# A two-layer hybrid attention trunk: projections of the next head pair move ahead of the gate, and scores that are not ready are passed over

## The chip, the core and the metric

The kernel runs on one core of one Trainium2 chip. The metric is the device time of one execution in microseconds (us); lower is better. The core has five instruction queues that run side by side and meet at semaphores: PE (TensorE, the matrix engine), DVE (VectorE), ACT (ScalarE), POOL (GpSimd) and SP (SyncE, which issues all DMAs here). Each queue runs its own instructions in the order in which they stand in the program.

## The reference, cut to what matters

Two layers of the following, on 1040 rows (16 learned meta tokens and 1024 inputs) of width 1024:

```python
hn = rmsnorm(h, norm_gain[l])
dq, dk, dv, dg, fq, fk, fv, ff, fg = jnp.split(hn @ w_in[l], split_points, axis=-1)
# four "diff" heads: two softmaxes per head, subtracted; q and k are rotated first
a = p[:, :, 0] - lam * p[:, :, 1]
do = rmsnorm(a @ dv, subln_gain[l]) * (1.0 - lam_init) * silu(dg)
# eight "fox" heads: causal softmax with a running sum of log-forget values as bias
log_f = jax.nn.log_sigmoid(ff + forget_bias[l])
cum_logf = jnp.cumsum(log_f, axis=1)
s = fq @ fk.T * scale + cum_logf[q] - cum_logf[k]
fo = (softmax(s) @ fv) * silu(fg)
h = h + concat([do, fo]) @ w_out[l]
```

## The kernel before

The rows are cut into 9 blocks and the blocks into 3 chunks of 336, 384 and 320 columns. The heads are worked in 8 pairs: pairs 0 to 3 are the diff heads, pairs 4 to 7 the fox heads. A layer runs on PE as two streams that are woven together:

- **Attention** (`attention`, `Unit`): for pair p and chunk c, scores (`scores`, PSUM tile `sc`), softmax on DVE and ACT (`e`, `mn`), transposes of the weights (`tp`, evicted by ACT and DVE as `ath` and `atl`), and the product with v (`po`). While the transposes and products of one unit run, the scores of the next unit `nx` are emitted between them.
- **Projections** (`fills`): units k, q, g (gate) and v, in the order of the string `ORDER`, which is cut by `|` into one segment for each pair. k0, for example, is the k projection of pair 0: three chunks of 24 matmuls each into a PSUM tile `pj`. There are two `pj` buffers. v2 also projects the 8 forget columns `ff`.

A matmul of two float32 matrices is made of three products of high and low parts, so every weight tile is loaded by DMA (`wst`), copied to `whi` (ACT or POOL) and subtracted to `wlo` (POOL or DVE). There are 4 buffers of `wst` and 8 each of `whi` and `wlo`; a v unit uses all 8, the others 4.

The order of PE's instructions is written out while the program is built: a planner in `layer` keeps an estimated clock `pe.t` and, each time that attention yields, emits projection steps in proportion to what is left of each stream. Attention names a key that must exist (`("k", p, c)`, say); if it does not, projection units are emitted until it does. A projection unit may yield `True`, which means that it has to wait for something: `k_unit` until the pair before the last has begun its scores, `q_unit` for chunk c until the scores of the pair before have used the buffer `ql` of that chunk. In that case `fills` takes the next gate out of the list and runs it as `other` in the place of the waiting unit, a step of 6 matmuls at a time; when the waiting unit can go on, `other` stays where it is until a unit waits again. The other engines' instructions are ordered by a scheduler of the build.

After the last step of v2, `log_forget` emits a chain of small DVE operations (and one exponential on ACT) on the forget columns, tile `ffz`, and returns the function `cumulate`. That one loads a triangular table with a DMA into a tile `tc` (3 buffers, of which the chain itself uses all three) and makes the running sum with matmuls `sc<-tc,ffz`, which need both the table and the chain's last result. `fills` calls it at a place of its own choice: before, when the unit behind v2 (k4) is finished. The unit `h` in the list works in the same way for the norms of the diff heads.

Of the kernel before, what the change touches and what calls it, by code (L numbers as in the profile page):

```python
# [42 lines left out]
LOP = [1, 1, 1, 1, 1, 1, 0, 0, 0, 1, 1, 0]  # L43


ORDER = ("k0 q0 k1 q1 | g0 k2 v1 q2 | g1 k3 q3 | g2 v2 k4 q4 | g3 k5 q5 | g4 v3 h k6 q6 | k7 q7 g5 | "
         "g6 g7")

START = "T0 S0 N0 x2 S1 T1 N1 v v v v v v S2 T2 N2 v v v v v v"

# [3 lines left out]

LS, LSC, LT, L1S, LROT, LFOX = ((1.9, 0.0033), (3.4, 0.0042)), 0.7, 2.4, 4.87, 8.0, 5.61
OT1, OT2, OT3, OW, OL = 2.46, 4.57, 2.54, 7.53, 4.52
CMAX, SLACK, RMIN, RMAX, STEP, FR0, FR1 = 3.17, 0.4, 0.03, 2.52, 2, 2, 2
COST = {"k": 11.4, "q": 11.4, "g": 11.4, "v": 25.7, "h": 0.0}
FADD = [0.0, 0.0, 0.0, 0.0, 0.0, 0.0, 0.0, 20.0]
# [25 lines left out]
def trunk_kernel(ctx, tc, x, meta, norm_gain, w_in, fbias, lq1, lk1, lq2, lk2,  # L85
# [87 lines left out]
    pe = Clock()  # L173
    const = {}
    when = {}
# [308 lines left out]
    def v_unit(l, u, acts, box):  # L484
        diff = u < 2
        v0 = (DV if diff else FV) + (u % 2) * 256
        cols = [(v0, v0 + 256)]
        n = 256
        ff = u == 2
        if ff:  # L490
            cols.append((FF, FF + 8))
            n = 264
        while u and box.get("vp", 0) < 2 * u - 1:
            yield True
        ws = load_w_all(w_in[l], cols)
        vt = [sb.tile([P, NB, 256], F32R, name="v", tag="v", bufs=3) for _ in range(2)]
        if ff:
            z = st("ffz", NB * 8, bufs=1)
            nc.vector.memset(z, 0.0)
        for j in range(NB):  # L500
            c = j // 3
            while acts[c] is None:
                yield True
            hi, lo = acts[c]
            sz = BE[j] - BS[j]
            pad = 64 if j == NB - 1 else 0
            o = BS[j] - CS[c] - pad
            m = sz + pad
            pt = proj_ps()
            i = 0  # L510
            for k in range(KT):
                wh, wl = ws[k]
                for a, b in ((hi, wh), (hi, wl), (lo, wh)):
                    mm(pt[:m, :n], a[:, k, o:o + m], b[:, :n], i == 0, i == 3 * KT - 1)
                    i += 1
                if k == 3:
                    yield
            for s in range(2):
                src = pt[pad:m, s * P:(s + 1) * P]
                if pad:  # L520
                    nc.gpsimd.memset(vt[s][0:pad, j, :].bitcast(F32), 0.0)
                if diff:
                    vh, vl = vt[s][pad:m, j, 0:P], vt[s][pad:m, j, P:2 * P]
                else:
                    src = src.rearrange("p (h d) -> p h d", h=2)
                    vv = vt[s][pad:m, j, :].rearrange("p (h x d) -> p h x d", h=2, x=2)
                    vh, vl = vv[:, :, 0, :], vv[:, :, 1, :]
                split(vh, vl, src, 1.0 if diff else 0.5)
            if ff:
                nc.vector.tensor_tensor(z[:sz, j * 8:(j + 1) * 8], pt[pad:m, 256:264],  # L530
                                        fb[:sz, l, :], ALU.add)
            box["v", 2 * u, j], box["v", 2 * u + 1, j] = vt
            when["v", 2 * u, j] = when["v", 2 * u + 1, j] = pe.t + 2.0
            if ff and j == NB - 1:
                box["lf"] = log_forget(l, z)
            yield

    def log_forget(l, z):

        n = NB * 8  # L540
        az = st("tc", CW)[:, :n]
        nc.vector.scalar_tensor_tensor(az, z, -1.0, z, ALU.mult, ALU.max)
        e = st("tc", CW)[:, :n]
        nc.scalar.activation(e, az, AF.Exp, scale=-1.0)

        d = st("tc", CW)[:, :n]
        nc.vector.tensor_scalar(d, e, 2.0, None, ALU.add)
        nc.vector.reciprocal(d, d)
        s = az
        nc.vector.tensor_tensor(s, e, d, ALU.mult)  # L550
        w = d
        nc.vector.tensor_tensor(w, s, s, ALU.mult)
        q = e
        nc.vector.tensor_scalar(q, w, 1.0 / 15, None, ALU.mult)
        for i in (13, 11, 9, 7, 5, 3):
            nc.vector.scalar_tensor_tensor(q, q, 1.0 / i, w, ALU.add, ALU.mult)
        nc.vector.scalar_tensor_tensor(q, q, 1.0, s, ALU.add, ALU.mult)
        nc.vector.tensor_scalar(z, z, 0.0, None, ALU.min)
        nc.vector.scalar_tensor_tensor(z, q, -2.0, z, ALU.mult, ALU.add)

        def cumulate():
            crow = big("cb", 2)
            upper = st("tc", CW)
            dma(out=upper[:, 0:P], in_=cst[:, C_U:C_U + P])
            for c in range(3):
                pt = proj_ps("sc")
                for j in range(3 * c, 3 * c + 3):
                    sz = BE[j] - BS[j]
                    o = BS[j] - CS[c]
                    mm(pt[:8, o:o + sz], z[:sz, j * 8:(j + 1) * 8], upper[:sz, :sz], True, True, 4)  # L570
                for j in range(3 * c, 3 * c + 3):
                    o = BS[j] - CS[c]
                    sz = BE[j] - BS[j]
                    prev = crow[:8, BS[j] - 1:BS[j]] if j else zero1[:8, :]
                    nc.vector.tensor_scalar(crow[:8, BS[j]:BE[j]], pt[:8, o:o + sz], prev, None,
                                            ALU.add)
            dma(out=cscr[l], in_=crow[:8, :])
        return cumulate


# [224 lines left out]
    def attention(l, box):  # L805
# [5 lines left out]
        def score(u, step):  # L811
# [7 lines left out]
                        dma(out=cb, in_=cscr[l, h:h + 1, :].to_broadcast([P, T]))  # L819
            u.score(*step)  # L820

        late = []
        todo = units[0].score_steps()
        yield 0.0, ("k", 0, 0)
# [4 lines left out]
        for i, u in enumerate(units):  # L829
            nx = units[i + 1] if i + 1 < len(units) else None  # L830
            todo = nx.score_steps() if nx else []
            free = EB - 3
            if nx and nx.diff:
                free = 2 * free - 1
            if nx and nx.p != u.p and not nx.diff:
                free = 0
            n = u.nblk
            seq = [("t", j) for j in range(TB)]
            for j in range(n):
                seq.append(("a", j))  # L840
                if j + TB < n:
                    seq.append(("t", j + TB))
            nt = 0
            yield u.ready, ("v", u.p, 0)
            box["vp"] = u.p
            for k, (what, j) in enumerate(seq):
                if late and pe.t >= late[0][0]:
                    late.pop(0)[1]()
                    yield 0.0, None
                if what == "t":  # L850
                    u.transp(j)
                    nt += 1
                else:
                    yield u.ev[j][2], ("v", u.p, j)
                    u.av(j)
                yield 0.0, None
                if todo and (nt == n or (free > 0 and nt >= FR0 and k % FR1 == FR1 - 1)):
                    free -= 1
                    yield 0.0, ("k", nx.p, nx.c)
                    yield pe.evicted[0], ("q", nx.p, nx.c)  # L860
                    score(nx, todo.pop(0))
                    yield 0.0, None
            for t0, f in late:
                yield t0, None
                f()
            late = u.finish()
            while todo:
                yield 0.0, ("k", nx.p, nx.c)
                yield pe.evicted[0], ("q", nx.p, nx.c)
                score(nx, todo.pop(0))  # L870
                yield 0.0, None
# [151 lines left out]
    def fills(l, acts, box, new):  # L1023

        unit = {"k": k_unit, "q": q_unit, "g": gate, "v": v_unit}
        todo = ORDER.replace("|", "").split()
        other = None
        while todo:
            u = todo.pop(0)
            now = head_norms(l, box) if u == "h" else unit[u[0]](l, int(u[1]), acts, box)  # L1030
            for r in now:
                if r and other is None:
                    g = next((x for x in todo if x[0] == "g"), None)
                    if g and u[0] != "v":
                        todo.remove(g)
                        other = gate(l, int(g[1]), acts, box)
                if r and other is not None:
                    r = next(other, "end")
                    if r == "end":
                        other, r = None, True  # L1040
                yield r
            if "lf" in box and u[0] not in "vh":
                box.pop("lf")()
            if other is not None and (not todo or todo[0][0] == "v"):
                yield from other
                other = None
# [67 lines left out]
    with tc.manual_schedule(engines={mybir.EngineType.PE}):  # L1114
        acts = [None] * 3
        box = {"done": {}, "sc_ok": set(), "fin": set(), "kept": 0, "sums": 0}
# [83 lines left out]
```

## Time and profile before

| | |
|---|---|
| time, median of 3 runs | 1607.41 us (1606.68 to 1609.51) |
| profiled execution: time, span | 1607.66 us, 1605.6 us |
| PE busy | 1487.7 us, 93% of the span |
| DVE, ACT, POOL busy | 1043.0, 828.6, 689.6 us |
| granted TensorE clock, mean of the span | 0.973 |

The span runs from the first to the last instruction; 2.1 us of the profiled time lie around it. The clock is granted as a share of 2.4 GHz. It takes one of two levels, 2.4 or 1.2 GHz, so a mean of 0.91 over a stretch says that 18% of it passed at 1.2 GHz, and at a steady stream of matmuls such a stretch does 9% less work.

### The profile page before, as it was taken

Reading aid. Unit: us, or ns where it says so; the run is one execution under the profiler, and the core shown is the slowest. Engines: PE = TensorE matmul, PEld = TensorE weight load, DVE = VectorE, ACT = ScalarE, POOL = GpSimd, SP = SyncE. Lnnn points to the kernel's source line nnn. Section 1 sums busy time; section 2 is a strip of 40 time slices with the busy share of each in tenths; the row PEclk is TensorE's granted clock in tenths of the full one; section 3 lists DMA queues with packets and bytes.
Section 4 is the critical chain, followed back from the end, with each engine's and each line's share of the span. In section 5 each row is a group of like instructions: output and inputs, shape, how many; then the busy total and the mean of one; then the engine's idle time right before and its main releaser. Section 6 shows DMA issues by size and latency. Waiting matters only on the chain. (4 is left out here: it accounts for less than half of the span.)

```text
span 1605.6 us, 30162 instructions
## 1 busy us (share of the span) xinstructions
PE 1487.7 (93%) x9932; PEld 1420.1 (88%) x9932; DVE 1043.0 (65%) x3024; ACT 828.6 (52%) x2067; POOL 689.6 (43%) x1125
## 2 busy tenths in 40 slices
PE   5988999999999999988998999899999999888997
PEld 4888989999999999887988899799999999886897
DVE  6488747866755575757655976586756555547564
ACT  6455545545654565543334654465556556446443
POOL 3353233404442445456846341442253344344674
PEclk9999999999999999998999999999999999999999
DMA  9252212223321324555434231332242222335454
GB/s 242 64 113 73 71 51 75 72 36 86 69 66 42 79 67 126 170 151 159 147 70 106 69 87 33 88 81 50 43 93 59 52 69 61 87 96 159 138 158 139
DMA packets 181725, 148.28 MB, mean 92 GB/s; under 512 B 19624, under 2 KB 177120, under 8 KB 181568
## 3 DMA queue, kind: packets, MB, share of 16 engines
q1 hardware_dynamic: 181568, 146.34, 34.6%
q8 instruction: 79, 1.29, 0.3%
q14 instruction: 78, 0.64, 0.1%
HBM read 117.70 MB, written 28.59 MB: 91 GB/s over the span
## 5 line engine op out<-in xcount | busy, mean ns | idle before, releaser
L179 PE MATMUL pj<-acth,whi 128*128 128x320 f32 (+2 forms) x1536 | 517.0, 337 | 22.9 <-ACT tc L416 7.6
L179 PE MATMUL pj<-acth,wlo 128*128 128x320 f32 (+2 forms) x1536 | 498.1, 324 | 2.7 <-POOL wlo L263 2.7
L179 PE MATMUL pj<-actl,whi 128*128 128x320 f32 (+2 forms) x1536 | 497.8, 324 | 0.0
L263 POOL TENSOR_TENSOR wlo<-wst,whi 128x256 fp32r<-128x256 f32 (+1 forms) x320 | 249.3, 788 | 244.0 <-ACT whi L259 216.3
L179 PEld LDWEIGHTS pj<-acth,whi 128*128 128x128 f32 x1536 | 295.9, 193 | 28.0 <-ACT tc L416 8.2
L179 PEld LDWEIGHTS pj<-acth,wlo 128*128 128x128 f32 x1536 | 295.2, 192 | 3.8 <-POOL wlo L263 3.2
L179 PEld LDWEIGHTS pj<-actl,whi 128*128 128x128 f32 x1536 | 293.9, 191 | 0.0
L660 ACT ACTIVATE e<-e,mn 80x80 f32<-80x80 f32 (+8 forms) x288 | 225.2, 782 | 124.2 <-DVE mn L652 121.6
L744 DVE TENSOR_TENSOR atl<-tp,ath 128x320 fp32r<-128x320 f32 (+8 forms) x432 | 191.5, 450 | 97.7 <-ACT ath L743 92.9
L743 ACT ACTIVATE ath<-tp 128x320 fp32r<-128x320 f32 (+8 forms) x432 | 167.6, 403 | 138.2 <-PE tp L183 131.1
L179 PE MATMUL sc<-kt,qq 128*128 128x296 f32 (+9 forms) x480 | 178.8, 375 | 25.2 <-DVE mn L652 17.3
L259 ACT ACTIVATE whi<-wst 128x256 fp32r<-128x256 f32 (+1 forms) x304 | 124.1, 415 | 150.4 <-DMA wst<-in_w_out_dram 50.7
L693 POOL TENSOR_SCALAR e<-e,rl 80x80 f32<-80x80 f32 (+2 forms) x144 | 110.8, 770 | 165.6 <-DVE rl L692 160.2
L183 PE MATMUL tp<-ident,e 128*128 128x128 f32 (+2 forms) x1080 | 180.7, 275 | 0.9 <-POOL e L693 0.8
L179 PE MATMUL po<-ath,v 128*128 128x256 f32 (+5 forms) x576 | 167.1, 331 | 13.2 <-ACT ath L743 9.9
L179 PE MATMUL pj<-whi,acth 128*128 128x256 f32 (+3 forms) x576 | 166.4, 289 | 6.7 <-DVE v L428 5.8
L179 PE MATMUL pj<-wlo,acth 128*128 128x256 f32 (+3 forms) x576 | 164.2, 285 | 2.1 <-POOL wlo L263 1.4
L179 PE MATMUL pj<-whi,actl 128*128 128x256 f32 (+3 forms) x576 | 163.8, 284 | 0.6 <-POOL actl L404 0.6
L179 PE MATMUL sc<-kt,ql 128*128 128x296 f32 (+9 forms) x480 | 159.7, 335 | 0.0
L179 PE MATMUL po<-atl,v 128*128 128x256 f32 (+5 forms) x432 | 136.8, 317 | 12.8 <-DVE atl L744 11.7
L183 PEld LDWEIGHTS tp<-ident,e 128*128 128x128 f32 (+2 forms) x1080 | 137.1, 140 | 7.0 <-POOL e L693 2.3
L179 PEld LDWEIGHTS sc<-kt,qq 128*128 128x128 f32 (+1 forms) x480 | 91.5, 191 | 37.7 <-DVE mn L652 23.8
(166 smaller groups left out, 2471.5 us busy)
## 6 DMA issues: line engine op xcount, KB each, us to landing
wst<-in_w_in_dram SPq DMA_DIRECT2D x256, 128.0 KB
wst<-in_w_out_dram SPq DMA_DIRECT2D x192, 128.0 KB
cb<-cscr SPq DMA_DIRECT2D x16, 520.0 KB
cb<-in_rope_dram SPq DMA_DIRECT2D x20, 320.0 KB
cb<-in_rope_dram SPq DMA_DIRECT2D x16, 384.0 KB
oscr<-ta SPq DMA_DIRECT2D x22, 192.0 KB
oscr<-ta SPq DMA_DIRECT2D x26, 160.0 KB
cb<-in_rope_dram SPq DMA_DIRECT2D x12, 336.0 KB
```

The lines of the kernel that those rows point to most:

```text
L179: nc.tensor.matmul(o, a, b, start=start, stop=stop)
L183: nc.tensor.transpose(o, a, idn)
L259: nc.scalar.activation(hi, sg_, AF.Copy)
L263: eng.tensor_tensor(lo, sg_, hi.bitcast(F32), ALU.subtract)
L660: nc.scalar.activation(e[rows, :ext], e[rows, :ext], AF.Exp, scale=-1.0, bias=mn[rows, len(pcs) - 1:len(pcs)], accum_out=l[rows, :])
L693: nc.gpsimd.tensor_scalar(e[rows, :ext], e[rows, :ext], r[rows, 0:1], 1.0, ALU.mult, ALU.mult)
L743: nc.scalar.activation(ah[:kz, n0:w], tp[:kz, n0:w], AF.Copy)
L744: nc.vector.tensor_tensor(al[:kz, n0:w], tp[:kz, n0:w], ah[:kz, n0:w].bitcast(F32), ALU.subtract)
```

## The change

`ORDER` now has k and q of the next pair first in each segment and the gate last; the units of each segment are the same, but for the place of the gate in it. In `attention`, a score of the next unit is emitted between transposes only when its k and q (and, for a fox pair, the running sum) are there by the planner's clock (`there`); if not, it is owed (`due`) and emitted later. `cumulate` is now called inside the loop over a unit's steps, when the planner's clock is past `box["lft"]`, which is set to `pe.t + LLF` when a v unit or `h` ends.

```diff
-ORDER = ("k0 q0 k1 q1 | g0 k2 v1 q2 | g1 k3 q3 | g2 v2 k4 q4 | g3 k5 q5 | g4 v3 h k6 q6 | k7 q7 g5 | "
-         "g6 g7")
+ORDER = ("k0 q0 k1 q1 | k2 q2 v1 g0 | k3 q3 g1 | k4 v2 q4 g2 | k5 q5 g3 | k6 q6 v3 h g4 | "
+         "k7 q7 g5 | g6 g7")
...
+LLF, LCUM = 8.0, 8.0
...
+            box["cum"] = True
+            when["cum"] = pe.t + LCUM
         return cumulate
...
+        def there(u):
+
+            return all(x in box and when.get(x, 0.0) <= pe.t + SLACK
+                       for x in (("k", u.p, u.c), ("q", u.p, u.c), "cum")[:2 if u.diff else 3])
...
-                if todo and (nt == n or (free > 0 and nt >= FR0 and k % FR1 == FR1 - 1)):
+                due += nt >= FR0 and k % FR1 == FR1 - 1
+                if todo and (nt == n or (free > 0 and due > 0)) and there(nx):
                     free -= 1
-                    yield 0.0, ("k", nx.p, nx.c)
-                    yield pe.evicted[0], ("q", nx.p, nx.c)
+                    due -= 1
+                    yield pe.evicted[0], None
                     score(nx, todo.pop(0))
                     yield 0.0, None
...
             while todo:
                 yield 0.0, ("k", nx.p, nx.c)
+                if not nx.diff:
+                    yield 0.0, "cum"
                 yield pe.evicted[0], ("q", nx.p, nx.c)
...
+                if "lf" in box and pe.t > box["lft"]:
+                    box.pop("lf")()
                 yield r
-            if "lf" in box and u[0] not in "vh":
-                box.pop("lf")()
+            if u[0] in "vh":
+                box["lft"] = pe.t + LLF
```

What the order of PE's instructions becomes is shown at two places of layer 1, and DVE's at one.

**First place, the end of v2 and the running sum.** PE before, at the last three matmuls of v2 (`pj`, 264 columns); the product, transpose and scores of pair 3 follow, and then k4:

```order
L179 MATMUL pj<-whi,acth_573 128x264
L179 MATMUL pj<-wlo,acth_573 128x264
L179 MATMUL pj<-whi,actl_574 128x264
L179 MATMUL po<-ath,v 128x384 x2
L179 MATMUL po<-atl,v 128x384
L183 MATMUL tp<-ident,e 128x128
L179 MATMUL sc<-kt,qq 128x488
```

The running sum stands about a hundred rows further on, behind the 72 matmuls of k4 and the first two products of pair 3's last unit, and ahead of q4:

```order
L179 MATMUL po<-ath,v 128x320 x2
L179 MATMUL po<-atl,v 128x320
L183 MATMUL tp<-ident,e 128x128 x3
L179 MATMUL sc<-tc,ffz 8x80
L179 MATMUL sc<-tc,ffz 8x128 x7
L179 MATMUL sc<-tc,ffz 8x64
L179 MATMUL pj<-acth_254,whi 128x336
```

PE now, at the same last three matmuls of v2:

```order
L181 MATMUL pj<-whi,acth_573 128x264
L181 MATMUL pj<-wlo,acth_573 128x264
L181 MATMUL pj<-whi,actl_574 128x264
L181 MATMUL sc<-tc,ffz 8x80
L181 MATMUL sc<-tc,ffz 8x128 x7
L181 MATMUL sc<-tc,ffz 8x64
L181 MATMUL po<-ath,v 128x256 x2
L181 MATMUL po<-atl,v 128x256
L181 MATMUL sc<-kt,qq 128x488
```

The running sum moved up to stand directly behind v2's last matmul: `box["lft"]` still held the value that v1 had set, so it was long past. Layer 2 has the same rows there.

DVE before, from the forget column of v2's last block (`ffz<-pj,fb`) into the chain of `log_forget` (rows on `ffz` and `tc` of 72 columns); rows on `e` and `mn` are a score's, `kt` is k4's eviction:

```order
L530 TENSOR_TENSOR ffz<-pj,fb 64x8
L652 ISA e,mn<-sc,dm,mn 128x488
L652 ISA mn 128x1
L542 SCALAR_TENSOR_TENSOR tc<-ffz 128x72
L558 TENSOR_SCALAR ffz<-ffz 128x72
L656 TENSOR_SCALAR e,mn<-sc 128x488
L882 SCALAR_TENSOR_TENSOR msv<-l_811 128x36
L547 TENSOR_SCALAR tc<-tc 128x72
```

DVE now, at the same place:

```order
L432 SCALAR_TENSOR_TENSOR v<-pj,v 64x2x64
L532 TENSOR_TENSOR ffz<-pj,fb 64x8
L544 SCALAR_TENSOR_TENSOR tc<-ffz 128x72
L560 TENSOR_SCALAR ffz<-ffz 128x72
L549 TENSOR_SCALAR tc<-tc 128x72
L550 RECIPROCAL tc<-tc 128x72
L552 TENSOR_TENSOR tc<-tc 128x72
L554 TENSOR_TENSOR tc<-tc 128x72
L556 TENSOR_SCALAR tc<-tc 128x72
L558 SCALAR_TENSOR_TENSOR tc<-tc 128x72 x6
L559 SCALAR_TENSOR_TENSOR tc<-tc 128x72
L561 SCALAR_TENSOR_TENSOR ffz<-tc,ffz 128x72
```

The other work that stood between the chain's links has moved behind it, and the first link follows the last eviction of v2 (`v<-pj`) at once.

**Second place, the first gate.** PE before, with the tiles' numbers, from the middle of the first gate chunk (`pj_1754`, of which 12 matmuls are done) over head sums, transposes and a score of pair 1:

```order
L179 MATMUL pj_1754<-actl0_255,whi_1736 128x336
L179 MATMUL sc_1767<-ones_77,ta_1660 128x1 x3
L183 MATMUL tp_1774<-ident_66,e_1507 80x128
L183 MATMUL tp_1782<-ident_66,e_1507 128x128
L179 MATMUL sc_1792<-kt_1165,qq_1469 80x256
L179 MATMUL sc_1792<-kt_1165,ql00_85 80x256
L179 MATMUL pj_1754<-acth0_254,whi_1742 128x336
```

PE now, at the same score and behind it; `pj_1823` is the first chunk of k2:

```order
L181 MATMUL pj_1754<-actl0_255,whi_1736 128x336
L181 MATMUL sc_1767<-ones_77,ta_1660 128x1 x3
L185 MATMUL tp_1774<-ident_66,e_1507 80x128
L185 MATMUL tp_1782<-ident_66,e_1507 128x128
L181 MATMUL sc_1792<-kt_1165,qq_1469 80x256
L181 MATMUL sc_1792<-kt_1165,ql00_85 80x256
L181 MATMUL pj_1823<-acth0_254,whi_1799 128x336
```

The gate chunk, half done, is no longer finished behind the score. It goes on only after all of k2 and the first chunk of q2 (`pj_2093`):

```order
L181 MATMUL pj_2093<-acth0_254,whi_2089 128x336
L181 MATMUL pj_2093<-acth0_254,wlo_2090 128x336
L181 MATMUL pj_2093<-actl0_255,whi_2089 128x336
L181 MATMUL pj_1754<-acth0_254,whi_1742 128x336
L181 MATMUL pj_1754<-acth0_254,wlo_1743 128x336
```

Until then one of the two `pj` buffers is taken by the waiting gate.

## Rows read from the trace of the kernel before

**Rows 1.** The page: span, busy time of PE, granted clock in 40 slices

```profile
span 1605.6 us, 30162 instructions
PE 1487.7 (93%) x9932; PEld 1420.1 (88%) x9932; DVE 1043.0 (65%) x3024; ACT 828.6 (52%) x2067; POOL 689.6 (43%) x1125
...
PEclk9999999999999999998999999999999999999999
```

**Rows 2.** PE's waits: who waited for whom, us in total, times, longest

```profile
PE sc L179 <- DVE mn L652: 17.3, 15, 3.8
```

**Rows 3.** Busy time by stretch: length, each engine, granted clock, DMA share, GB/s

```profile
core 0: us, PE busy (x) PEld busy (x) DVE busy (x) ACT busy (x) POOL busy (x), PEclk, DMA share, GB/s
146.00:175.00 29.00, 27.35 (x188) 26.91 (x189) 19.38 (x57) 15.13 (x41) 12.55 (x21) 1.00 0.32 87
228.00:246.00 18.00, 13.24 (x77) 11.96 (x76) 11.59 (x34) 8.03 (x23) 11.85 (x16) 0.91 0.40 102
1007.00:1027.00 20.00, 12.84 (x77) 11.83 (x76) 11.07 (x30) 8.39 (x24) 12.26 (x20) 0.91 0.43 93
1387.00:1424.00 37.00, 27.80 (x173) 26.03 (x172) 10.82 (x33) 11.55 (x33) 12.07 (x25) 0.94 0.28 82
359.00:385.00 26.00, 25.37 (x176) 24.04 (x176) 22.05 (x67) 14.17 (x35) 10.99 (x17) 1.00 0.30 66
664.00:700.00 36.00, 26.23 (x139) 22.56 (x139) 26.89 (x69) 20.21 (x48) 14.54 (x23) 0.81 0.60 169
1464.00:1500.00 36.00, 30.87 (x181) 27.96 (x180) 27.80 (x65) 21.07 (x49) 17.92 (x26) 0.86 0.45 128
```

**Rows 4.** PE in time order, layers 1 and 2, at q2's last chunk: start, duration

```profile
232.11 0.41 PE L179 MATMUL pj<-acth,whi 128*128 128x320 f32 x1 [2.10 <-ACT tc L416]
...
241.95 0.90 PE L179 MATMUL po<-ath,v 128*128 128x320 f32 x2 [2.50 <-ACT ath L743]
...
1013.53 0.63 PE L179 MATMUL pj<-acth,whi 128*128 128x320 f32 x1 [5.45 <-ACT tc L416]
...
1023.24 0.56 PE L179 MATMUL po<-ath,v 128*128 128x320 f32 x2 [1.36 <-ACT ath L743]
```

**Rows 5.** ACT in time order ahead of the wait that ends at 1013.53

```profile
1011.96 0.42 ACT L259 ACTIVATE whi<-wst 128x256 fp32r<-128x256 f32 x1 [4.58 <-DMA wst<-in_w_in_dram]
...
1013.05 0.43 ACT L416 ACTIVATE tc<-pj 128x320 f32<-128x320 f32 x1
```

**Rows 6.** PE in time order at the gates of layer 2

```profile
1388.90 0.38 PE L179 MATMUL pj<-acth,whi 128*128 128x320 f32 x1 [1.61 <-DVE ql L430]
...
1395.24 0.44 PE L179 MATMUL pj<-acth,whi 128*128 128x384 f32 x1 [1.05 <-DVE tc L615]
1398.99 0.61 PE L179 MATMUL po<-ath,v 80*128 80x320 f32 x1 [2.44 <-DVE ta L782]
...
1407.64 0.41 PE L179 MATMUL pj<-acth,whi 128*128 128x320 f32 x1 [1.17 <-DVE tc L615]
...
1422.11 0.44 PE L179 MATMUL pj<-acth,whi 128*128 128x384 f32 x1 [2.50 <-DVE gs L615]
```

**Rows 7.** PE in time order: v2's last matmul and the running sum, layer 1

```profile
362.58 0.28 PE L179 MATMUL pj<-whi,actl 128*128 128x264 f32 x1
...
381.01 2.04 PE L179 MATMUL sc<-tc,ffz 80*8 80x80 f32 x18
```

**Rows 8.** DVE in time order: first and last operation of the chain

```profile
366.99 0.17 DVE L530 TENSOR_TENSOR ffz<-pj,fb 64x8 f32<-64x8 f32 x1
...
376.32 0.72 DVE L559 SCALAR_TENSOR_TENSOR ffz<-tc,ffz 128x72 f32<-128x72 f32 x1
```

**Rows 9.** Busy time on the tile `tc` alone, from the forget column to the DMA

```profile
367.16:376.05 8.89, 0.00 (x0) 0.00 (x0) 3.28 (x12) 0.25 (x1) 0.00 (x0) 1.00 0.29 84
```

**Rows 10.** SP in time order: issue of the table's DMA

```profile
376.05 0.34 SPq L564 DMA_DIRECT2D tc<-in_cst_dram  x1
```

**Rows 11.** The chain that ended last: two of its waits for a DMA

```profile
1544.59 3.39 DMA wst<-in_w_out_dram
...
1549.34 2.23 DMA wst<-in_w_out_dram
```

More of the change, by code (lines that the diff above doesn't have):

```diff
@@ L534, in v_unit, with log_forget @@
             if ff and j == NB - 1:
-                box["lf"] = log_forget(l, z)
+                box["lf"] = log_forget(l, z, box)
             yield
-    def log_forget(l, z):
+    def log_forget(l, z, box):
         n = NB * 8
@@ L842, in attention @@
                     seq.append(("t", j + TB))
-            nt = 0
+            nt = due = 0
             yield u.ready, ("v", u.p, 0)
```

## The prediction

> **What bounds the kernel now.** I read the page first: PE is busy for 1487.7 of 1605.6 us and the clock is near its upper level in nearly every slice [rows 1]. PE is the bound. Whatever makes it wait, or start again at the lower clock, is paid in full; what the other engines do costs only where PE stands still for it. The waits in total come next: the largest sort is 17.3 us in 15 pieces, scores behind the softmax on DVE [rows 2], and no sort is large. So the question is where the 118 us of idle PE lie. Reading PE in the order of time, I kept three stretches that the new order touches, and took their sums from the busy time by stretch [rows 3]:
>
> - q2 of layer 1, 228 to 246: idle 18.00 - 13.24 = 4.8 us, clock 0.91.
> - q2 of layer 2, 1007 to 1027: idle 7.2 us, clock 0.91.
> - the gates of layer 2, 1387 to 1424: idle 9.2 us, clock 0.94.
>
> At the place where the running sum goes, 359 to 385, PE idles for 0.6 us in 26 at the full clock: there is no slack to win there, only to lose.
>
> **Part 1, q2 leaves the queue behind v1: a gain.** Before, q2 stands behind v1, and the first score of pair 2 needs it at once, so all three chunks are drawn in one burst. The third waits until the first is evicted by ACT (2.10 and 5.45 us), and products behind it wait for ACT again (2.50 and 1.36) [rows 4]. ACT is late because a copy of the next weights stands ahead of the eviction and waits 4.58 us for its DMA [rows 5]; v1 had held all 8 weight buffers. Now q2's chunks lie one by one between gates and attention, ahead of v1. The idle time and the lost clock (9% of 18 and of 20 us) are 4.8 + 1.6 + 7.2 + 1.8 = 15.4 us. But some unit still follows v1, now k3, and its weights come as late: part of the wait moves to the transposes and scores beside k3. I take four fifths, 12.3 us, between half (7.7) and all of it.
>
> **Part 2, the half-done gate of layer 2 goes: a gain.** In layer 2 before, PE's order has g5 begun as `other` beside q7 and left with a quarter done until after g7. It keeps one `pj` buffer, so q7, g6 and g7 have one: each new chunk waits until the one before it is evicted, 1.61, 1.05, 1.17 and 2.50 us [rows 6]. In the new order g5 is finished early and q7, g6, g7 have both buffers. Idle 9.2 and lost clock 6% of 37, 2.2: together 11.4 us, which I take whole.
>
> **Part 3, a half-done gate at another place: a loss, in both layers.** As the order of PE shows, g0 now stands half done while k2 and the first chunk of q2 run. Per layer three chunks then start on the single buffer, six in all. In [rows 6] such a start cost 1.05 to 2.50 us with little or nothing between; here a transpose, a product or a score stands between, and a rotated k needs only one ACT copy to free the buffer. I take 0.6 us each, 3.6 us, between 0 and 9.6 (1.6 each, the mean in [rows 6]).
>
> **Part 4, the running sum directly behind v2: the largest loss.** `sc<-tc,ffz` needs two things. The chain's result: before, v2's last matmul ends at 362.86 [rows 7], its forget column is added at 367.16, and the chain ends at 377.04 [rows 8]. The table: its DMA is issued at 376.05 [rows 10], only when the chain gives a `tc` buffer back, 13.2 us behind v2's last matmul. Before, PE hid all of it under k4 and reached the sum at 381.01 without a wait [rows 7]. Now PE arrives at once. What it waits for is the sum of three pieces.
>
> - From v2's last matmul to the forget column: 4.3 us before. By ACT's new order the last copy of v2 stands behind the exponential of the score ahead of it, but that score ends earlier than before; I take 4.5.
> - The chain up to the free buffer: 8.9 us before, of which its own operations on `tc` are 3.3 on DVE and 0.25 on ACT [rows 9]. Unbroken, as DVE's new order has it, and with the hand-overs: 4.2.
> - The DMA: waits of this kind are 2.23 to 3.39 us [rows 11], with 128 KB. The table is half of that; 2.3.
>
> That is 11.0 us per layer. Lower bound: the chain alone and the shorter DMA, 3.3 + 2.2 = 5.5. Upper bound: 13.2 as before, and the longer DMA, 16.6. Behind such a pause PE starts at 1.2 GHz; a wait of 5.45 us went with a loss of 1.8 us of clock (9% of 20) [rows 3, 4], and I add the same. So 2 x (11.0 + 1.8) = 25.6 us. Queued behind the waiting matmul on PE are a product, the last score of pair 3 and q4; everything else waits for those, so nothing fills the pause.
>
> The Trainium skill (DMA: Bandwidth & Descriptors, Anatomy of one DMA) fits a DMA as 2.0 us and its bytes at 436 GB/s; as an estimate that is 2.15 us for 64 KB, by which the term would be 25.3 us and the result 0.3 us less. The same page (Rules for kernel authors) says to issue a DMA early and to wait for it late, which speaks against this place; the rows of before, where 5 us lie between issue and use, agree.
>
> **Part 5, the rest.** The units and so the matmuls of a layer are the same: PE's busy time stays. In 146 to 175 DVE is busy for 19.4 of 29 us [rows 3]; k2 and q2 take the place of a gate there, with evictions of five and more DVE passes a chunk against one. DVE stays under 29, and v1's weights are converted a little later: 2 us for both layers, 0 to 4. At the end of attention layer 2 lost its late g5 as a filler, so its last unit will look as in layer 1: idle 9.8 and clock 19% of 36 (6.8) there, against 5.1 and 5.0 here [rows 3]. That is 6.5 us at most; I take 5. The scores that are passed over add no instruction; beside those of pair 2 (part 1) hardly a score waited for its q or k before, so I cost the rule itself at nothing: the transposes and products that now come first are work that PE had to do anyway. Were these not ready, a score's wait would take their place, a few tenths of a us.
>
> **The sum.** -12.3 - 11.4 + 3.6 + 25.6 + 2 + 5 = +12.5 us on the profiled 1607.66: 1620.2. The median of the runs is 0.25 lower. I say 1620.
>
> **Rivals.**
>
> - *Faster: the pause is short.* Place: the 18 matmuls of the running sum. With its two pauses left out, the sum stands at -13.1 + 0 = -13.1 us, so the kernel is faster by over 0.2% (3.2 us) if a pause with its clock costs under 4.9 us. At 4.0 it gives 1602.6. For it: DVE's new order is unbroken. Against: the chain and its DMA alone are 5.5.
> - *No change: the pause is 5.5 to 8 us with little loss of clock*, or the gains are whole and parts 3 and 5 nothing. Pauses of 6.5 give 1607.6.
> - *Slower still: the pause is as long as the way was before*, 16.6 + 1.8, since ACT's queue may wait for weights there as in [rows 5], and half of part 1 stays. -7.7 - 11.4 + 36.8 + 10.6 = +28.3: 1636.
> - *PE passes the waiting matmuls by.* Then the change is worth -13.1: 1594.6. In [rows 4] no matmul ran in the 5.45 us, though attention stood behind; I count it into the chance of faster. The Trainium skill (TensorE: Matmul & The Clock Gate, The mechanism) says that matmuls start in strict order; by that rule this rival gets next to nothing.
>
> **Chances.** Forecast (4 to 22 us slower) 0.57; still slower 0.17; no change 0.14; faster 0.12. What a measurement of this kernel can tell from no change is about 0.2%, 3.2 us: faster 0.12, same 0.14, slower 0.74. The range leaves out about half of faster and the far end of still slower: 1604 to 1633. The forecast's own range is 1611 to 1629.
>
> **What would show it.** A wait of about 11 us ahead of the first `sc<-tc,ffz` in each layer, put down to the table's DMA or to `ffz`, and the lower clock behind it. No wait of over 2 us at q2's last chunk, nor at the gates of layer 2. Small waits, ended by ACT `tc`, ahead of the second and third chunk of k2 and the first of q2. If the running sum starts within 5 us of v2's last matmul, part 4 is wrong and the kernel is faster; if waits for ACT appear beside k3, part 1 was moved rather than removed.

## The result, and the profile after

| | before | after |
|---|---|---|
| time, median of 6 runs each, same chip | 1607.31 us (1605.65 to 1609.64) | 1625.20 us (1621.53 to 1627.88) |
| ratio after / before, 95% interval | | 1.0108 (1.0090 to 1.0126) |
| profiled execution: time, span | 1607.66 us, 1605.6 us | 1622.79 us, 1620.9 us |

The changed kernel is 1.1% slower. The forecast was 1620.0 us, with a range of 1604 to 1633. The page of after, in the lines that answer to [rows 1]:

```profile
span 1620.9 us, 30144 instructions
PE 1486.1 (92%) x9932; PEld 1419.7 (88%) x9932; DVE 1056.3 (65%) x3024; ACT 829.6 (51%) x2067; POOL 688.5 (42%) x1125
...
PEclk9999999998999999988999999999799999998999
```

PE's busy time is within 1.6 us of before; its idle time (span less busy time) is 16.9 us longer. In the clock, the tenth and the 29th slice fell from 9 in [rows 1] to 8 and 7: a quarter and 70% of the way through, where v2 ends in each layer. (The 18th and the 37th, at the ends of attention, are at 8.) PE's waits in total (who waited for whom, us, times, longest), after:

```profile
PE sc L181 <- DMA tc<-in_cst_dram: 33.8, 2, 17.5
PE po L181 <- DVE atl L748: 17.9, 17, 3.1
PE sc L181 <- DVE mn L656: 11.5, 11, 3.8
```

The sort that was largest, scores behind `mn`, fell from 17.3 [rows 2] to 11.5 us. A new sort of two pieces is twice as large as any before. PE in time order, at v2's last matmul and the running sum, layers 1 and 2 (answers to [rows 7]):

```profile
354.90 0.28 PE L181 MATMUL pj<-whi,actl 128*128 128x264 f32 x1
371.48 3.43 PE L181 MATMUL sc<-tc,ffz 80*8 80x80 f32 x18 [16.30 <-DMA tc<-in_cst_dram]
...
1145.60 0.28 PE L181 MATMUL pj<-whi,actl 128*128 128x264 f32 x1
1163.41 3.41 PE L181 MATMUL sc<-tc,ffz 80*8 80x80 f32 x18 [17.53 <-DMA tc<-in_cst_dram]
```

PE stands still for 16.30 and 17.53 us. Behind that, the same 18 matmuls take 3.4 us instead of 2.04 [rows 7]. What they wait for is seen on the other three queues. DVE after, layer 1, the links of the chain (answers to [rows 8]):

```profile
360.18 0.17 DVE L532 TENSOR_TENSOR ffz<-pj,fb 64x8 f32<-64x8 f32 x1
360.38 0.23 DVE L544 SCALAR_TENSOR_TENSOR tc<-ffz 128x72 f32<-128x72 f32 x1
...
362.21 0.25 DVE L549 TENSOR_SCALAR tc<-tc 128x72 f32<-128x72 f32 x1 [1.36 <-ACT tc L546]
...
366.25 0.23 DVE L561 SCALAR_TENSOR_TENSOR ffz<-tc,ffz 128x72 f32<-128x72 f32 x1
```

ACT after, the same stretch (a longer exponential, `e<-e,mn` of the score, stands between the first two rows; `v<-pj` is the copy of v2's last block, `tc<-tc` the chain's exponential):

```profile
357.29 0.42 ACT L261 ACTIVATE whi<-wst 128x256 fp32r<-128x256 f32 x1 [1.80 <-DMA wst<-in_w_in_dram]
359.13 0.42 ACT L261 ACTIVATE whi<-wst 128x256 fp32r<-128x256 f32 x1 [0.33 <-DMA wst<-in_w_in_dram]
359.57 0.27 ACT L428 ACTIVATE v<-pj 64x128 fp32r<-64x128 f32 x1
361.60 0.42 ACT L261 ACTIVATE whi<-wst 128x256 fp32r<-128x256 f32 x1 [1.76 <-DMA wst<-in_w_in_dram]
361.93 0.25 ACT L546 ACTIVATE tc<-tc 128x72 f32<-128x72 f32 x1
```

SP after, layer 1, and then the table's issue in layer 2 (answers to [rows 10]):

```profile
354.58 9.57 SPq L254 DMA_DIRECT2D wst<-in_w_in_dram  x8
365.98 0.34 SPq L566 DMA_DIRECT2D tc<-in_cst_dram  x1
...
1157.03 0.34 SPq L566 DMA_DIRECT2D tc<-in_cst_dram  x1
```

In layer 1 the pause is made of 5.0 us from v2's last matmul (it ends at 355.18) to the forget column, 5.8 us on to the issue of the table's DMA, and 5.5 us until PE goes on. In layer 2 the first two come to 11.15 us together and the DMA to 6.4; there one more load (`ta<-oscr`, issued at 1157.42) follows 0.4 us behind the table.

The stretches, after (length, each engine, granted clock, DMA share, GB/s): from the table's issue to the sum in both layers, all that lies behind the first gate up to pair 3 in both layers, the gates of layer 2, g0 with k2 and q2 in both layers, and the ends of attention in layers 1 and 2:

```profile
365.98:371.48 5.50, 0.00 (x0) 0.03 (x1) 0.46 (x2) 0.00 (x0) 0.00 (x0) 0.50 0.33 59
1157.03:1163.41 6.38, 0.00 (x0) 0.03 (x1) 0.46 (x2) 0.00 (x0) 0.00 (x0) 0.50 0.57 79
...
193.00:300.00 107.00, 103.71 (x730) 100.44 (x730) 79.92 (x235) 58.69 (x149) 36.17 (x52) 1.00 0.26 59
984.00:1090.00 106.00, 103.13 (x733) 100.46 (x732) 78.64 (x237) 58.64 (x147) 36.11 (x57) 1.00 0.24 60
...
1408.00:1457.00 49.00, 49.00 (x343) 47.44 (x342) 26.58 (x86) 26.21 (x71) 23.74 (x49) 1.00 0.35 103
...
140.00:193.00 53.00, 50.24 (x323) 48.89 (x322) 42.61 (x114) 27.93 (x70) 24.76 (x35) 0.97 0.34 92
931.00:984.00 53.00, 49.15 (x321) 47.91 (x321) 39.84 (x109) 26.48 (x68) 24.75 (x39) 0.97 0.37 89
...
657.00:718.00 61.00, 53.34 (x312) 48.40 (x312) 41.65 (x112) 32.38 (x76) 26.13 (x42) 0.89 0.51 156
1457.00:1517.00 60.00, 47.58 (x285) 43.35 (x284) 43.43 (x102) 32.06 (x75) 24.68 (x43) 0.89 0.45 132
```

These are the stretches of before: first the two behind the first gate up to pair 3, then those beside the last four above, in the same order:

```profile
193.00:300.00 107.00, 99.22 (x670) 95.87 (x668) 75.05 (x218) 53.71 (x134) 34.64 (x52) 0.98 0.24 66
976.00:1090.00 114.00, 104.09 (x705) 100.98 (x705) 79.20 (x240) 58.99 (x150) 43.50 (x69) 0.99 0.29 68
...
140.00:193.00 53.00, 50.13 (x355) 49.12 (x353) 40.48 (x115) 29.31 (x78) 20.11 (x28) 1.00 0.32 86
922.00:976.00 54.00, 51.65 (x367) 50.37 (x366) 40.45 (x119) 28.32 (x77) 19.25 (x31) 1.00 0.30 82
...
657.00:713.00 56.00, 46.23 (x274) 41.79 (x273) 38.22 (x99) 29.28 (x70) 23.72 (x40) 0.88 0.57 161
1449.00:1505.00 56.00, 48.15 (x292) 43.38 (x291) 40.53 (x102) 33.14 (x77) 30.02 (x47) 0.91 0.47 136
```

Behind the first gate 3.3 and 2.9 us of idle time are left, at the full clock. The longest wait there stands beside k3, in both layers (1.01 and 1.03 us), and ends with DVE's eviction of v:

```profile
259.09 0.42 PE L181 MATMUL pj<-acth,whi 128*128 128x336 f32 x1 [1.01 <-DVE v L430]
```

At the gates of layer 2 no idle time is left at all.

### The profile page after: what moved, and what is told of

The parts are those of the page before. It is cut to its first block, busy times and chain, and to the rows that moved or that the text cites. A ratio compares the mean times of both kernels' runs of the same rounds, so it can differ in the third digit from the quotient of the medians.

```text
span 1620.9 us, 30144 instructions
## 1 busy us (share of the span) xinstructions
PE 1486.1 (92%) x9932; PEld 1419.7 (88%) x9932; DVE 1056.3 (65%) x3024; ACT 829.6 (51%) x2067; POOL 688.5 (42%) x1125
## 4 chain that ended last, share of the span: by engine, by line
PE 57%; DVE 11%; DMA 8%; issue 6%; POOL 3%; ACT 2%; SPq 0%; DVEq 0%; POOLq 0%; ACTq 0%
PE pj L181 36%; PE sc L181 8%; PE po L181 7%; PE tp L185 6%; DMA wst<-in_w_out_dram 3%; DMA wst<-in_w_in_dram 2%; DVE wlo L265 2%; POOL wlo L265 1%; DVE e L656 1%; DMA oscr<-ta 1%; DMA actl<-oscr 1%; DVE actl L430 1%; DVE atl L748 1%; DMA tc<-in_cst_dram 1%; DVE kt L430 1%
## 5 line engine op out<-in xcount | busy, mean ns | idle before, releaser
L181 PE MATMUL sc<-kt,qq 128*128 128x296 f32 (+9 forms) x480 | 175.6, 368 | 15.8 <-DVE mn L656 11.5
L265 DVE TENSOR_TENSOR wlo<-wst,whi 128x256 fp32r<-128x256 f32 (+1 forms) x128 | 88.5, 696 | 62.4 <-POOL whi L263 53.0
```

Of the source, the lines that this page charges most:

```text
L181: nc.tensor.matmul(o, a, b, start=start, stop=stop)
L265: eng.tensor_tensor(lo, sg_, hi.bitcast(F32), ALU.subtract)
```

## The experiments

Each was timed in turns with the kernel before on one chip; "before" had medians of 1604.5 to 1605.6 us in these jobs, so ratios are compared, not times.

**1. The running sum behind the next unit.** The changed kernel with the old place of the call:

```diff
-                if "lf" in box and pe.t > box["lft"]:
-                    box.pop("lf")()
                 yield r
-            if u[0] in "vh":
-                box["lft"] = pe.t + LLF
+            if "lf" in box and u[0] not in "vh":
+                box.pop("lf")()
```

> The changed kernel, with the running sum emitted where the old code did, when the unit behind v2 (now q4) is finished; everything else of the change stays. Theory (the pause directly behind v2 is the loss, the rest of the change is a gain): the waits of 16.3 and 17.5 us ahead of the running sum, seen in the changed kernel, go, with 1.5 us each of lost clock behind them; the time falls by 34 to 38 us to 1587 to 1592, some 1% faster than the kernel before. Rival (the pause only gathers waits that would arise anyway, since DVE and the weights are late there): waits of some 5 to 10 us per layer turn up ahead of q4 and the transposes of pair 3, and the time stays at 1605 to 1615.

Ratio 0.9919 (0.9896 to 0.9942), median 1593.43 us. The sum in layer 1, in PE's time order:

```profile
377.45 2.04 PE L181 MATMUL sc<-tc,ffz 80*8 80x80 f32 x18
```

There is no wait ahead of it, and its matmuls take 2.04 us again; in layer 2 the wait is 0.40 us. So the list and the rule on scores are a gain of 0.8%, 13.0 us, and the early sum costs 1.0108 / 0.9919 = 1.019, some 30 us (26 to 35, an estimate from the two intervals). The theory holds, but the 34 to 38 us that it expected were too many. This version beats both kernels.

**2. The early sum alone, in the kernel before.**

```diff
-            if "lf" in box and u[0] not in "vh":
+            if "lf" in box and u[0] != "h":
                 box.pop("lf")()
```

> The kernel before with one part of the change alone: the running sum is emitted directly behind v2 (one score of pair 3 lies between); the list of units and the rule for scores are the old ones. Theory: two waits of 13 to 18 us ahead of the running sum, time 1607 + 30 to 38 = 1637 to 1645. Rival (the new list of units makes the pause long, by what it queues ahead of the table's DMA): in the old list the waits are 6 to 10 us and the time is 1620 to 1628.

Ratio 1.0138 (1.0113 to 1.0164), median 1628.82 us.

```profile
374.14 3.72 PE L179 MATMUL sc<-tc,ffz 80*8 80x80 f32 x18 [9.60 <-DMA tc<-in_cst_dram]
```

The early sum makes the kernel before slower too, but the pauses are 9.6 us each, not 13 to 18: the theory fell and the rival holds. The table was issued at 372.13, so its DMA took 2.0 us here. In that time the DMA engines moved (GB/s is last):

```profile
372.13:374.14 2.01, 0.00 (x1) 0.03 (x1) 0.46 (x2) 0.00 (x0) 0.00 (x0) 0.50 0.13 33
```

2.01 us at 33 GB/s are 66 KB, the table's 64 KB alone (128 x 128 float32, 65.5 thousand bytes): no weights were left in flight. The time rose by 22 us; the two waits are 19.2 of it, and the slower matmuls behind them (3.72 us against 2.04) another 3.4.

**3. The table loaded early.** The changed kernel, with the table in a tile of its own that v2 loads before its chain exists:

```diff
+            box["tab"] = st("msr", P, bufs=1)
+            dma(out=box["tab"], in_=cst[:, C_U:C_U + P])
...
-            upper = st("tc", CW)
-            dma(out=upper[:, 0:P], in_=cst[:, C_U:C_U + P])
+            upper = box["tab"]
```

> The changed kernel, with the triangular table loaded at the start of v2 into a buffer that nothing else holds then, so that the running sum waits for the chain's result alone. In the changed kernel the table's DMA was issued 10.8 us behind v2's last matmul and PE went on 5.4 us (layer 1) and 6.3 us (layer 2) later. Theory (the pause is the chain, then the DMA): the chain's last operation ends about 1 us behind the issue of the DMA, so each wait falls by 4.4 to 5.3 us to about 12, and the time by some 9 us to 1616. Rival (the DMA is not what PE waits for last; the chain is): the waits stay at 15 to 17 us and the time at 1625.

Ratio 1.0049 (1.0032 to 1.0066). The wait, in total over both layers:

```profile
PE sc L181 <- DVE ffz L563: 23.4, 2, 11.8
```

The DMA's part is 33.8 - 23.4 = 10.4 us, 5.2 in each layer. What remains, 11.7 us, is the front and the chain, and the wait now ends with the chain's last operation.

**4. The delay that the code names.** `LLF` is 8 us, but `box["lft"]` still held the value that v1 had set. Here the old value is cleared when a v unit or `h` starts:

```diff
+            if u[0] in "vh":
+                box["lft"] = 1e9
             now = head_norms(l, box) if u == "h" else unit[u[0]](l, int(u[1]), acts, box)
```

> The changed kernel, with the mark for the running sum cleared when v2 begins, so that the sum comes when the planner's clock is 8 us past the end of v2: behind the first two chunks of q4 and some transposes. Theory: by then about 8 us of work lie between v2 and the sum, and the way from v2's last matmul to the table takes 13 us or more once DVE has other work between the links, and 2 to 6 us for the DMA: each wait shrinks from 16 to 18 to about 8 to 10 us, and the time falls by 14 to 18 us to 1607 to 1611. Rival (evictions of q4 on DVE push the chain back by as much as PE gains): the waits stay at 14 us or more and the time at 1620 to 1625.

Ratio 1.0042 (1.0024 to 1.0061). The sum in layers 1 and 2:

```profile
371.71 3.72 PE L181 MATMUL sc<-tc,ffz 80*8 80x80 f32 x18 [4.59 <-DMA tc<-in_cst_dram]
...
1160.18 3.72 PE L181 MATMUL sc<-tc,ffz 80*8 80x80 f32 x18 [10.78 <-DMA tc<-in_cst_dram]
```

The stale value explains that the sum stands directly behind v2, but 8 us of work ahead of it don't cover the way either. The time fell by less than expected, since the wait of layer 2 is still 10.78 us.

**5. The list alone**, in the kernel before (the two lines of `ORDER` of the diff, nothing else).

> The kernel before with the new list ORDER alone: scores are still emitted when they fall due, whether or not their q and k are there, and the running sum stands behind k4 or q4 as before. The kernel after with its sum at the old place gained 0.8% (ratio 0.992). Theory: that gain is the list's (q2 leaves the queue behind v1, the half-done gate of layer 2 goes), and the rule on scores is worth nothing: ratio 0.990 to 0.995, no wait at the gates of layer 2. Rival: the rule makes the gain, since with the old rule a due score pulls all chunks of a k or q out at once in the new list too: ratio 0.998 to 1.003, with waits ahead of the last chunk of q2 as before.

Ratio 0.9956 (0.9939 to 0.9972). The gates of layer 2 wait for nothing here either:

```profile
1390.00:1440.00 50.00, 50.00 (x345) 48.11 (x344) 25.52 (x83) 25.16 (x68) 21.45 (x44) 1.00 0.41 118
```

The list makes a gain by itself, of about half the size of experiment 1. Part of the difference is not the rule on scores: in layer 2 the running sum, at its old place, comes too early for the table here.

```profile
1157.15 3.06 PE L179 MATMUL sc<-tc,ffz 80*8 80x80 f32 x18 [2.65 <-DMA tc<-in_cst_dram]
```

The wait and the slower matmuls are 3.7 us, 0.23%.

**6. The rule on scores alone**, with the old list and the old place of the sum.

> The old list with the new rule: a score whose q or k is not there is passed over; the running sum is called at the old place. Theory: hardly a score meets a missing q or k apart from pair 2, so little changes: ratio 0.997 to 1.001; the half-done gate of layer 2 and its waits of 1.0 to 2.5 us stay. Rival: the rule alone brings the gain of the kernel whose sum stood behind the next unit: ratio 0.990 to 0.994.

Ratio 0.9995 (0.9981 to 1.0009). The waits at the gates of layer 2 are still there, of 1.60, 1.05 and 2.31 us among them; the first:

```profile
1389.17 0.38 PE L181 MATMUL pj<-acth,whi 128*128 128x320 f32 x1 [1.60 <-DVE ql L432]
```

With the old list the rule is worth nothing. Experiments 1 and 5 differ by 0.4%, and their intervals meet at their ends; 0.2% of that is the wait for the table in experiment 5. What is left for the rule with the new list lies within the noise, so whether it is worth anything there isn't settled.

**7. The sum 20 us later, and the table early.** Experiments 3 and 4 together, with `LLF` at 20.

> The kernel after with the running sum 20 us of planned time behind v2 (the stale mark cleared) and its table loaded at the start of v2 instead of at the call. Theory: both pieces of the pause, the chain and the table's DMA, are then covered: no wait of over 1 us ahead of the sum, ratio 0.988 to 0.993, as with the sum behind the next unit. Rival: the sum's place matters in itself (its 18 short matmuls, what is emitted behind it): ratio 0.997 or more with no wait ahead of the sum.

Ratio 0.9937 (0.9917 to 0.9958). No wait ahead of the sum. With the pause gone no effect of the place is seen: this one and experiment 1 agree within their intervals.

**8. The table issued by another engine**, in the changed kernel:

```diff
-            dma(out=upper[:, 0:P], in_=cst[:, C_U:C_U + P])
+            nc.scalar.dma_start(out=upper[:, 0:P], in_=cst[:, C_U:C_U + P])
```

> The kernel after, but the table's DMA is issued by ACT's queue instead of SP's; nothing else is moved. In the kernel after it took 5.4 and 6.3 us from issue to the sum, behind three weight loads that SP issued 2 to 4 us ahead of it. Theory: it stands behind those loads in the same queue, so by another queue it takes 2.0 to 3.0 us, the pause is 12.5 to 14.5 us, and the time falls by 6 to 9 us: ratio to the kernel before 1.005 to 1.007. Rival: the transfers share the same engines and slow each other, whatever queue they came from: the pause stays at 16 to 17.5 us and the ratio at 1.010 to 1.012.

Ratio 1.0131 (1.0110 to 1.0152). ACT's issue of it in layer 1:

```profile
370.88 0.39 ACTq L566 DMA_DIRECT2D tc<-in_cst_dram  x1
```

And the sum on PE:

```profile
376.34 3.62 PE L181 MATMUL sc<-tc,ffz 80*8 80x80 f32 x18 [16.27 <-DMA tc<-in_cst_dram]
```

The table still takes 5.5 us. My theory of one queue in which it stands behind the weights fell. The Trainium skill (DMA: Bandwidth & Descriptors, Issuing engines are not separate DMA queues) says that DMAs of all issuing engines run on the same 16 DMA engines and interleave; this run agrees with it.

**9. v2 ahead of k4**, so that the weights ahead of the table are those of k4 and q4:

```diff
-... | k4 v2 q4 g2 | ...
+... | v2 k4 q4 g2 | ...
```

> The kernel after with v2 ahead of k4 in the list (v2 k4 q4 g2 in place of k4 v2 q4 g2), nothing else changed; the running sum still stands directly behind v2. The 8 weight loads ahead of the table's DMA are then those of k4 and q4, not those of q4 and the gate g2. In the kernel after, the loads ahead of the table moved at 54 GB/s and the table landed 5.4 and 6.3 us behind its issue; with the old list and k4, q4 ahead it took 2.0 us. Theory: it depends on which weights stand ahead, the gate's are the slow ones: the DMA takes 2.0 to 3.0 us here, the pause is 10 to 13 us, the ratio to the kernel before 1.003 to 1.008. Rival: it depends on how many loads were issued just ahead and on idle engines in the pause: the DMA takes 5 us or more, the pause is 15 to 18 us, ratio 1.009 to 1.013.

Ratio 1.0137 (1.0117 to 1.0157). SP's issues in layer 1:

```profile
347.20 7.30 SPq L254 DMA_DIRECT2D wst<-in_w_in_dram  x8
357.75 0.34 SPq L566 DMA_DIRECT2D tc<-in_cst_dram  x1
```

The sum on PE:

```profile
359.71 3.72 PE L181 MATMUL sc<-tc,ffz 80*8 80x80 f32 x18 [10.78 <-DMA tc<-in_cst_dram]
```

The stretch in which the weights moved, up to the table's issue, and that from its issue to the sum (GB/s is last):

```profile
352.00:357.70 5.70, 0.00 (x0) 0.00 (x0) 4.28 (x15) 1.52 (x5) 2.02 (x4) 0.50 0.38 94
357.75:359.71 1.96, 0.00 (x0) 0.03 (x1) 0.46 (x2) 0.00 (x0) 0.00 (x0) 0.50 0.14 33
```

The weights move at 94 GB/s, the table lands 1.96 us behind its issue, and the pauses shrink to 10.8 and 10.5 us, as expected. But this doesn't show that it depends on which weights stand ahead. 1.96 us at 33 GB/s are 65 KB, the table alone: all eight loads were issued by 354.5, 3.2 us ahead of the table, and had landed. In the kernel after, the last was issued by 364.2, 1.8 us ahead, and 5.50 us at 59 GB/s are 325 KB, five times the table: the rest are weights still in flight. The edit changed both, the weights and what was in flight, and the rival (loads issued just ahead) fits as well. On the time the theory missed: the kernel is no faster than after. The 12.5 us that the pauses lost stand elsewhere: PE's busy time is 1495.2 us (+9.1), and its waits for `atl` are 22.1 us (+4.2). Why the same matmuls are longer in this order stays open; experiment 6 has 1494.7 us of busy time at the time of the kernel before.

**10. The weight copies off ACT.** Experiment 3, with the 8 weight copies behind v2 made by POOL:

```diff
-        if HIA[i]:
+        quiet[0] -= 1
+        if HIA[i] and quiet[0] < 0:
             nc.scalar.activation(hi, sg_, AF.Copy)
...
                 box["lf"] = log_forget(l, z, box)
+                quiet[0] = 8
```

> The kernel with the table loaded at the start of v2 (pauses of 11.6 and 11.8 us, ended by the chain), and in it the 8 weight copies behind v2 (of q4 and g2) all made by POOL, none by ACT. In the kernel after, ACT's copy of v2's last block and the chain's exponential each stood behind a weight copy that waited 0.3 to 1.8 us for its DMA. Theory: these waits lengthen the front and the chain; without them the pauses are 8.5 to 10.3 us and the ratio to the kernel before is 1.001 to 1.004 (against 1.005). Rival: ACT's long exponential of the score and the chain's DVE operations set the length: pauses of 11 to 12 us, ratio 1.004 to 1.007.

Ratio 1.0015 (1.0001 to 1.0028). The wait in total:

```profile
PE sc L181 <- DVE ffz L567: 17.7, 2, 8.9
```

23.4 - 17.7 = 5.7 us less, and the ratio fell by 0.34%, 5.5 us. The theory held: ACT's short operations stood behind copies that waited for weights, 2.8 us in each layer.

**11. Other columns in g2's place**, in the changed kernel:

```diff
-        g0 = (DG if p < 4 else FG) + (p % 4) * P
+        g0 = FK if p == 2 else (DG if p < 4 else FG) + (p % 4) * P
```

> The kernel after, but the gate g2 loads other columns of the weights: those of k4 instead of its own (so the gate of pair 2 is computed from the wrong weights); every instruction, its place and its size are the same. In the kernel after, the table's DMA took 5.4 and 6.3 us behind g2's loads, which moved at 49 to 63 GB/s. Theory: those columns are slow to read, and with k4's the table lands 2.0 to 3.0 us behind its issue, the pauses are 12.5 to 14 us, ratio to the kernel before 1.004 to 1.008. Rival: the rate comes from when and how the loads are issued (three in a row, just ahead of the table), whatever their address: the DMA still takes 5 us or more, the pauses are 16 to 18 us, ratio 1.009 to 1.013.

Ratio 1.0145 (1.0124 to 1.0165). The table's issue in layer 1:

```profile
373.34 0.34 SPq L566 DMA_DIRECT2D tc<-in_cst_dram  x1
```

The stretches in which the weights moved, ahead of it and beside it, in both layers:

```profile
368.00:376.00 8.00, 0.00 (x0) 0.00 (x0) 3.79 (x13) 0.57 (x2) 2.08 (x3) 0.50 0.27 54
1164.00:1171.00 7.00, 0.00 (x0) 0.00 (x0) 2.48 (x11) 0.00 (x0) 0.00 (x0) 0.50 0.54 51
```

The sum starts at 378.27, 4.9 us behind the issue. The theory fell: with the columns of k4 the weights move at 54 and 51 GB/s too. It isn't the address of the columns.

## Why the prediction came out as it did

The direction, the mechanism and the range held. The parts, by the stretches above:

| part | forecast, us | measured, us |
|---|---|---|
| 1: q2 leaves the queue behind v1 | -12.3 | -14.8: idle and lost clock 21.0 before, 6.2 now, behind the first gate up to pair 3 |
| 2: the half-done gate of layer 2 | -11.4 | -11.4: PE is busy for 49.00 of 49.00 us |
| 3, and the first 2 us of 5: g0, k2, q2, v1 | +5.6 | +4.6: 1.4 more idle time, and 3% of the clock in 2 x 53 us |
| 4: the running sum | +25.6 | +36.6: idle 33.8, and 2 x 1.4 for the slower matmuls |
| 5: the ends of attention | +5 | +4: idle and clock +6.1 in layer 2, -2.1 in layer 1 |
| sum | +12.5 | +19.0 |

The spans differ by 15.3 us. Of the 3.7 us between, 3.3 lie ahead of the change: the first score of layer 1 starts at 87.81 against 91.10 in the profile of before. All other runs have it at 89.0 to 93.3, so that is scatter between executions. The measured column is a rough one: its stretches don't hold the same matmuls before and after (in part 3, 355 and 323 in layer 1), and don't cover the whole span. Experiment 1 puts part 4 at some 30 us rather than 36.6; where the difference comes back no run shows.

That the median lies only 5 us from the forecast is in part luck: part 4 was 11.0 us too small, and parts 1, 3 and 5 came out 4.5 us better than forecast.

**Parts 1 and 2** held, part 2 to the size and part 1 with 2.5 us to spare. The fifth of part 1 that was to move to k3 didn't come in that form: the longest wait there (1.01 and 1.03 us) ends with DVE's eviction of v, and those that end with the weights are 0.16 and 0.64 us. In part 2 experiment 6 shows the waits with the old list, and experiment 5 shows them gone with the new one alone.

**Part 3** was right on what stands where, and the cost came elsewhere: where I had looked for ACT there are no waits of note, and one wait of 2.60 us for the gate's own eviction on DVE at q2's second chunk in layer 2, with a stretch at 1.2 GHz behind it (granted clock 0.81 from 975 to 984):

```profile
975.35 0.69 PE L181 MATMUL pj<-acth,whi 128*128 128x384 f32 x1 [2.60 <-DVE tc L619]
```

**Part 4** had the right mechanism, on the right queue and with the right releaser, and was mis-sized. It said 4.5 + 4.2 + 2.3 = 11.0 us a layer; layer 1 has 5.0 + 5.8 + 5.5 = 16.3.

- *The DMA, 2.3 forecast, 5.5 and 6.4 measured.* This is the larger miss. I took the price from waits for single transfers [rows 11] and didn't ask what SP had issued just ahead. Three of the eight weight loads were issued in the 3.6 us before the table (at 362.4 to 363.8), and were still in flight when the table joined: of the 325 KB moved from its issue to the sum, the table is a fifth. Experiment 3 puts the price at 5.2 us a layer; where nothing else is in flight it is 2.0 us (experiments 2 and 9, layer 1), and with a change of issuing engine or of columns it stays at 4.9 us and more (8 and 11). The Trainium skill (DMA: Bandwidth & Descriptors, Anatomy of one DMA — SWDGE (gpsimd) path) has a fit, made on DMAs that GpSimd issues, that gives 2.15 us as an estimate for 64 KB, and the prediction took it for this DMA, which SP issues. Experiments 2 and 9 come near it with 2.0 us; the changed kernel doesn't.
- *The front and the chain, 8.7 forecast, 10.8 and 11.15 measured.* I had assumed the chain unbroken since DVE's order has it so. It is broken on ACT: its one exponential stands behind a weight copy that waits 1.76 us for its DMA, and in the front the score's exponential, with the copy of v2's last block behind it, stands behind one that waits 1.80. Experiment 10 takes those copies away, and PE's whole wait is then 8.8 and 8.9 us, which is the forecast's size.
- *The clock, 1.8 forecast, 1.4 measured*: the sum's matmuls take 3.4 us against 2.04, at a granted clock of 0.68 from 371.48 to 376.00. Behind the shorter pauses of experiments 2 and 9 they take 3.72.

So the pause became that of the rival "still slower", 16.6 us, by the ACT waits that it named and by a DMA that it took for 3.4. The time stayed in the forecast's own range since that rival also gave back half of part 1, which didn't happen.

**Part 5**, the rule at nothing: experiment 6 agrees for the old list; for the new one it isn't settled, but what experiments 1 and 5 leave for it is small.

**The rival that PE passes by** fell: no matmul runs in 16.30 us, though attention's products stood behind. **The short pause** fell with experiment 2: even where the DMA takes 2.0 us, PE waits 9.6.

What the change was worth without its one wrong place is experiment 1: a gain of 0.8%, against 13.1 us in the forecast's sum with its pauses left out.

## What to carry to other kernels

A matmul that waits stops everything behind it on PE. Before moving one up, add up its inputs' way from the last producer to the last landing, on all queues, and leave that much PE work ahead of it; here the way is 9 to 18 us. The sum behind the next unit waits for 0 to 2.65 us a layer (experiments 1 and 5), while the sum at once costs some 30 us in all.

The price of a small DMA is read from the place where it will stand, not from a transfer elsewhere: look at what was issued in the few us before it and hasn't landed. Nothing but its destination tied this table to the chain, so it can be loaded long before.

A delay kept in a variable that is set once holds only if the variable is cleared: print where the instructions went, and compare with what the constant says.

## What was not expected of the hardware

Weight loads of 128 KB move at two rates: 94 GB/s ahead of the table in experiment 9, and 54 in experiment 11 at the same kind of place; 54 GB/s is also found in the kernel before, while PE was busy throughout:

```profile
378.00:386.00 8.00, 8.00 (x62) 7.25 (x61) 6.04 (x17) 3.07 (x8) 1.86 (x3) 1.00 0.28 54
```

So idle engines are not the cause, and neither are the columns (experiment 11). Full DMA engines are not either: in layer 1 they are busy for 0.27 and 0.28 of such stretches, against 0.38 at 94 GB/s. What sets the rate stays open. A 64 KB load that is issued into such a stretch takes 4.9 to 7.0 us, in place of 2.0 with nothing else in flight; the 7.0 is from layer 2 of experiment 8, issued at 1161.93 with the sum at 1168.93.
